# A weighted sum of two experts' rows: all transfers in one queue, in a fixed order

## The chip, the cores and the metric

The kernel runs on one core of a Trainium2 chip. The metric is the device time in microseconds (us), as the median of several executions. The span in a profile is the time from the first to the last instruction of one profiled execution, and is a little shorter than the device time.

Five engines can work side by side on a core. Three matter here: VectorE (DVE in the profile), ScalarE (ACT), and SyncE (SP), which computes nothing and issues transfers. A transfer (DMA) between the large memory (HBM, "dram" in the profile) and the on-chip memory (SBUF, 128 partitions) is put into the queue of the engine that issues it, and is carried out by the core's 16 DMA engines. An instruction that issues a transfer first waits until what it needs is there: a load until its buffer is free, a store until its result is computed. While it waits, the instructions behind it on the same engine wait too.

## The reference

```python
batch, seq, hidden, n_experts, k = 16, 1024, 512, 8, 2
expert_outputs   # (16, 1024, 2, 512) float32
combine_weights  # (16, 1024, 2)      float32

def reference(expert_outputs, combine_weights):
    weights = combine_weights[..., np.newaxis]
    return np.sum(expert_outputs * weights, axis=2).astype(np.float32)
```

There are 16 x 1024 = 16,384 tokens. Each has two rows of 512 numbers, one from each of two experts, and two weights; the output row is the weighted sum. 67.1 MB are read and 33.6 MB are written.

## The kernel before

Each of the 128 partitions takes 128 tokens. They are worked in eleven tiles: ten of 12 tokens per partition (J) and one of 8 (LAST). A full tile is 128 x 12 x 1024 numbers, 6.29 MB to load; its result is half of that, 3.15 MB to store. The last tile is 4.19 MB to load and 2.10 MB to store. The result is written over the first half of the tile's own buffer, so that a buffer is free for the next load only when its store has landed. There are four buffers (`bufs=4`); tile g + 4 uses the buffer of tile g.

```python
J, LAST = 12, 8
main = per - LAST            # per = 128 tokens per partition
last = main // J             # 10: tiles 0 to 9 are full, tile 10 is the short one
wpool = ctx.enter_context(tc.tile_pool(name="w", bufs=1))
ipool = ctx.enter_context(tc.tile_pool(name="in", bufs=4))
wt = wpool.tile([P, per * k], dt)
# ... the weights are loaded by two small transfers, on SyncE's and ScalarE's queue

for g in range(last + 1):
    et = ipool.tile([P, J, k * h], dt)
    ot = et.rearrange("p j f -> p (j f)")[:, 0 : J * h].rearrange("p (j f) -> p j f", f=h)
    t0, c = g * J, J if g < last else LAST
    nc.sync.dma_start(out=et[:, 0:c], in_=eo(t0, c))                 # L67, the load
    if g < last - 1:                                                 # tiles 0 to 8
        wb = wt[:, g * J * k : (g + 1) * J * k].unsqueeze(2).to_broadcast([P, J * k, h])
        ek = et.rearrange("p j (k h) -> p (j k) h", k=k)
        nc.vector.tensor_tensor(out=ek, in0=ek, in1=wb, op=mult)     # L72
        nc.vector.tensor_tensor(out=ot, in0=et[:, :, 0:h], in1=et[:, :, h : 2 * h], op=add)  # L73
        nc.scalar.dma_start(out=o(t0, c), in_=ot)                    # L74, the store, ScalarE's queue
        continue

    for i in range(c):                                               # tiles 9 and 10
        t = t0 + i
        nc.scalar.activation(                                        # L80, first row times its weight
            out=et[:, i, 0:h], in_=et[:, i, 0:h], func=copy, scale=wt[:, 2 * t : 2 * t + 1]
        )
        if g == last:                                                # tile 10
            nc.vector.scalar_tensor_tensor(...)                      # L84, second row times weight, plus first
    if g < last:                                                     # tile 9
        # ... x1 is the tile's second rows, w1 their weights
        nc.vector.tensor_tensor(out=x1, in0=x1, in1=w1.to_broadcast([P, c, h]), op=mult)  # L95
        nc.vector.tensor_tensor(out=ot, in0=et[:, :, 0:h], in1=x1, op=add)                # L96
    nc.sync.dma_start(out=o(t0, c), in_=ot[:, 0:c])                  # L97, the last two stores, SyncE's queue
```

So there are eleven loads in SyncE's queue, nine stores in ScalarE's, and two stores in SyncE's behind all loads. A framework sets the waits between the instructions.

Of the kernel before, what the change touches and what calls it, by code (L numbers as in the profile page):

```python
# [1 line left out]

# [4 lines left out]


@with_exitstack
def kernel(  # L10
    ctx: ExitStack,
    tc: tile.TileContext,
    expert_outputs: bass.AP,
    combine_weights: bass.AP,
    out: bass.AP,
):

    nc = tc.nc  # L20
    b, s, k, h = expert_outputs.shape
    assert k == 2
    n = b * s
    P = nc.NUM_PARTITIONS
    per = n // P
    assert per * P == n
    J, LAST = 12, 8
    main = per - LAST
    assert main % J == 0
    eo = expert_outputs.rearrange("b s k h -> (b s) (k h)")  # L30
    cw = combine_weights.rearrange("b s k -> (b s) k")
    o = out.rearrange("b s h -> (b s) h")

    def rows(x):

        a = x[0 : P * main, :].rearrange("(p t) f -> p t f", p=P)
        b = x[P * main : n, :].rearrange("(p t) f -> p t f", p=P)
        return lambda t, c: a[:, t : t + c, :] if t < main else b[:, t - main : t - main + c, :]

    eo, cw, o = rows(eo), rows(cw), rows(o)  # L40

    dt = mybir.dt.float32
    mult = mybir.AluOpType.mult
    add = mybir.AluOpType.add
    copy = mybir.ActivationFunctionType.Copy

    last = main // J

    wpool = ctx.enter_context(tc.tile_pool(name="w", bufs=1))
    ipool = ctx.enter_context(tc.tile_pool(name="in", bufs=4))  # L50

    wt = wpool.tile([P, per * k], dt)

    for eng, t, c in ((nc.sync, 0, main), (nc.scalar, main, LAST)):
        eng.dma_start(  # L55
            out=wt[:, k * t : k * (t + c)].rearrange("p (t k) -> p t k", k=k), in_=cw(t, c)
        )

    warm = wpool.tile([P, 1], dt)
    nc.scalar.activation(out=warm, in_=nc.const_aps.tensor(1.0, (P, 1), dt), func=copy)  # L60

    for g in range(last + 1):
        et = ipool.tile([P, J, k * h], dt)

        ot = et.rearrange("p j f -> p (j f)")[:, 0 : J * h].rearrange("p (j f) -> p j f", f=h)
        t0, c = g * J, J if g < last else LAST
        nc.sync.dma_start(out=et[:, 0:c], in_=eo(t0, c))  # L67
        if g < last - 1:

            wb = wt[:, g * J * k : (g + 1) * J * k].unsqueeze(2).to_broadcast([P, J * k, h])  # L70
            ek = et.rearrange("p j (k h) -> p (j k) h", k=k)
            nc.vector.tensor_tensor(out=ek, in0=ek, in1=wb, op=mult)  # L72
            nc.vector.tensor_tensor(out=ot, in0=et[:, :, 0:h], in1=et[:, :, h : 2 * h], op=add)  # L73
            nc.scalar.dma_start(out=o(t0, c), in_=ot)  # L74
            continue


        for i in range(c):
            t = t0 + i
            nc.scalar.activation(  # L80
                out=et[:, i, 0:h], in_=et[:, i, 0:h], func=copy, scale=wt[:, 2 * t : 2 * t + 1]
            )
            if g == last:
                nc.vector.scalar_tensor_tensor(  # L84
                    out=ot[:, i, :],
                    in0=et[:, i, h : 2 * h],
                    scalar=wt[:, 2 * t + 1 : 2 * t + 2],
                    in1=et[:, i, 0:h],
                    op0=mult,
                    op1=add,  # L90
                )
        if g < last:
            w1 = wt.rearrange("p (t k) -> p t k", k=k)[:, t0 : t0 + c, 1:2]
            x1 = et[:, :, h : 2 * h]
            nc.vector.tensor_tensor(out=x1, in0=x1, in1=w1.to_broadcast([P, c, h]), op=mult)  # L95
            nc.vector.tensor_tensor(out=ot, in0=et[:, :, 0:h], in1=x1, op=add)  # L96
        nc.sync.dma_start(out=o(t0, c), in_=ot[:, 0:c])  # L97


# [1 line left out]
_INS = ['expert_outputs', 'combine_weights']  # L101
_OUTS = [((16, 1024, 512), 'float32')]


# [23 lines left out]
```

## Time and profile before

| | before |
|---|---|
| device time, median of three (lowest to highest) | 240.05 us (239.09 to 240.25) |
| the profiled execution: device time; span | 239.26 us; 237.5 us |
| VectorE busy | 194.0 us (82%), 28 instructions |
| ScalarE busy | 14.0 us (6%), 22 instructions |
| moved by DMA | 100.80 MB, mean 424 GB/s over the span |
| a full load, median from issue to landing | 29.9 us |
| a store in ScalarE's queue, median from issue to landing | 33.2 us |

An engine's busy time is the time in which it works on instructions; issuing a transfer is not counted. For transfers there are two ways to look. "From issue to landing" is the whole time that one transfer takes, the time spent behind and beside others included. The share of the DMA engines tells how full the 16 of them are in a stretch of time, whoever issued what. In a line of groups, "L72" is a line of the kernel's file, "et<-et,wt" what is written and read, "x9" the count, and then come the busy time in all and the mean in ns of one.

### The profile page before, as it was taken

To read this page: it belongs to the slowest core of one execution; us is meant where nothing else is said; L and a number is where in the kernel's file an instruction comes from. 1 tells how busy PE (TensorE), PEld (TensorE's weight loads), DVE (VectorE), ACT (ScalarE), POOL (GpSimd) and SP (SyncE) were. 2 spreads that over 40 slices of the span, in tenths; PEclk is the share of its full clock that TensorE was granted. 3 is DMA by queue.
4 is the path that set the end of the run, shared out by engine and by line. 5 is a ranking of instruction groups with operands and counts; after the bars stand their busy time and mean duration, and the time that the engine had idled before them with its cause. 6 is when DMAs were issued, how large, how long until landed. Compare 5 with 4: busy or idle time off the path is not lost.

```text
span 237.5 us, 153 instructions
## 1 busy us (share of the span) xinstructions
DVE 194.0 (82%) x28; ACT 14.0 (6%) x22; POOL 0.2 (0%) x4
## 2 busy tenths in 40 slices
DVE  0008999999999999999999879969996998785710
ACT  2000000000000000000000000000000000740800
POOL 0000000000000000000000000000000000000000
DMA  8999999889899999999898999999998989999997
GB/s 287 397 488 439 397 414 505 381 364 522 356 439 431 430 464 464 397 397 505 356 522 364 439 431 430 464 464 397 397 505 356 513 368 443 447 414 442 422 417 309
DMA packets 3456, 100.80 MB, mean 424 GB/s; under 512 B 512, under 2 KB 640, under 8 KB 640
## 3 DMA queue, kind: packets, MB, share of 16 engines
q1 hardware_dynamic: 2016, 72.48, 71.2%
q10 hardware_dynamic: 1440, 28.32, 27.7%
HBM read 67.24 MB, written 33.55 MB: 424 GB/s over the span
## 4 chain that ended last, share of the span: by engine, by line
DMA 59%; DVE 33%; ACT 2%; DVEq 0%; ACTq 0%; issue 0%; SPq 0%
DMA et<-in_expert_outputs_dram 30%; DMA out_dram<-et 29%; DVE et L72 22%; DVE et L73 11%; ACT et L80 2%; DVE et L84 1%; DVEq L123 0%; ACTq L123 0%; SPq L55 0%; SPq L67 0%; DVEq L72 0%; ACTq L80 0%
## 5 line engine op out<-in xcount | busy, mean ns | idle before, releaser
L72 DVE TENSOR_TENSOR et<-et,wt 128x12288 f32<-128x12288 f32 x9 | 116.6, 12955 | 25.3 <-DMA et<-in_expert_outputs_dram 25.3
L73 DVE TENSOR_TENSOR et<-et 128x6144 f32<-128x6144 f32 x9 | 59.0, 6558 | 0.3
L80 ACT ACTIVATE et<-et,wt 128x512 f32<-128x512 f32 x20 | 12.5, 708 | 210.0 <-DMA et<-in_expert_outputs_dram 210.0
L84 DVE SCALAR_TENSOR_TENSOR et<-et,wt 128x512 f32<-128x512 f32 x8 | 5.6, 747 | 3.9 <-ACT et L80 3.7
L95 DVE TENSOR_TENSOR et<-et,wt 128x6144 f32<-128x6144 f32 x1 | 6.6, 6558 | 2.2 <-DMA et<-in_expert_outputs_dram 2.2
L96 DVE TENSOR_TENSOR et<-et 128x6144 f32<-128x6144 f32 x1 | 6.6, 6558 | 0.9 <-ACT et L80 0.9
L60 ACT ACT_TABLE_LOAD x1 | 1.3, 1283 | 1.2 <-PEq L112 1.2
L60 ACT ACTIVATE warm<-const-float32-1.0 128x1 f32<-128x1 f32 x1 | 0.2, 203 | 0.0
L112 POOL MEMSET const-bfloat16-1.0<- 128x1 bf16 x1 | 0.1, 102 | 0.0
L112 POOL MEMSET const-uint8-127<- 128x1 uint8 x1 | 0.1, 102 | 0.0
L112 POOL MEMSET const-float32-0.0<- 128x1 f32 x1 | 0.1, 99 | 0.2 <-issue 0.2
L112 POOL MEMSET const-float32-1.0<- 128x1 f32 x1 | 0.1, 99 | 0.0
## 6 DMA issues: line engine op xcount, KB each, us to landing
et<-in_expert_outputs_dram SPq DMA_DIRECT2D x10, 6144.0 KB, 29.9
out_dram<-et ACTq DMA_DIRECT2D x9, 3072.0 KB, 33.2
et<-in_expert_outputs_dram SPq DMA_DIRECT2D x1, 4096.0 KB, 25.1
out_dram<-et SPq DMA_DIRECT2D x1, 3072.0 KB, 14.7
out_dram<-et SPq DMA_DIRECT2D x1, 2048.0 KB, 10.0
wt<-in_combine_weights_dram SPq DMA_DIRECT2D x1, 120.0 KB, 2.1
wt<-in_combine_weights_dram ACTq DMA_DIRECT2D x1, 8.0 KB, 2.3
```

Source lines behind the costliest of these rows:

```text
L60: nc.scalar.activation(out=warm, in_=nc.const_aps.tensor(1.0, (P, 1), dt), func=copy)
L72: nc.vector.tensor_tensor(out=ek, in0=ek, in1=wb, op=mult)
L73: nc.vector.tensor_tensor(out=ot, in0=et[:, :, 0:h], in1=et[:, :, h : 2 * h], op=add)
L80: nc.scalar.activation(out=et[:, i, 0:h], in_=et[:, i, 0:h], func=copy, scale=wt[:, 2 * t : 2 * t + 1])
L84: nc.vector.scalar_tensor_tensor(out=ot[:, i, :], in0=et[:, i, h : 2 * h], scalar=wt[:, 2 * t + 1 : 2 * t + 2], in1=et[:, i, 0:h], op0=mul ...
L95: nc.vector.tensor_tensor(out=x1, in0=x1, in1=w1.to_broadcast([P, c, h]), op=mult)
L96: nc.vector.tensor_tensor(out=ot, in0=et[:, :, 0:h], in1=x1, op=add)
L112: nc = _bacc.Bacc("TRN2", target_bir_lowering=False, num_devices=1)
```

## The change

All loads and stores go into SyncE's one queue. The program issues four loads (one for each buffer), then the stores of tiles 0 and 1, and from there a load and a store by turns. The load of tile g + 3 stands behind the store of tile g; the buffer that it fills was that of tile g - 1, whose store stands two transfers earlier. `keep_in_program_order` keeps the framework from reordering the transfers. The computation is the same. The purpose is that transfers run one after another in an order that is known, each with the DMA engines to itself, and that a load waits for a store that has landed by the time it is to run, instead of one that still shares the DMA engines with other loads.

```diff
-    J, LAST = 12, 8
+    J, LAST, BUFS = 12, 8, 4
...
-    ipool = ctx.enter_context(tc.tile_pool(name="in", bufs=4))
+    ipool = ctx.enter_context(tc.tile_pool(name="in", bufs=BUFS))
...
-    for g in range(last + 1):
+    tiles = {}
+
+    def load(g):
+        t0, c = g * J, J if g < last else LAST
         et = ipool.tile([P, J, k * h], dt)
 
         ot = et.rearrange("p j f -> p (j f)")[:, 0 : J * h].rearrange("p (j f) -> p j f", f=h)
-        t0, c = g * J, J if g < last else LAST
-        nc.sync.dma_start(out=et[:, 0:c], in_=eo(t0, c))
+        tiles[g] = (t0, c, et, ot)
+        tc.keep_in_program_order(nc.sync.dma_start(out=et[:, 0:c], in_=eo(t0, c)))
+
+    def store(g):
+        t0, c, et, ot = tiles[g]
+        tc.keep_in_program_order(nc.sync.dma_start(out=o(t0, c), in_=ot[:, 0:c]))
+
+    def compute(g):
+        t0, c, et, ot = tiles[g]
         if g < last - 1:
...
-            nc.scalar.dma_start(out=o(t0, c), in_=ot)
-            continue
+            return
...
-        nc.sync.dma_start(out=o(t0, c), in_=ot[:, 0:c])
+
+    for g in range(BUFS):
+        load(g)
+    for g in range(last + 1):
+        compute(g)
+        store(g)
+        if 1 <= g <= last - BUFS + 1:
+            load(g - 1 + BUFS)
```

Nothing of the computation of a tile is changed but its place in the file: it now stands in `compute`.

## The prediction

> **What bounds the kernel now.** I read the page's slices and its part on DMA queues first, because this kernel moves 100.8 MB and multiplies little. The lines are the busy tenths and the GB/s of 40 equal slices, and then one line for each DMA queue: packets, MB, and the share of the span in which the 16 DMA engines worked for it. q1 is SyncE's queue, q10 ScalarE's.
>
> ```profile
> DVE  0008999999999999999999879969996998785710
> DMA  8999999889899999999898999999998989999997
> q1 hardware_dynamic: 2016, 72.48, 71.2%
> q10 hardware_dynamic: 1440, 28.32, 27.7%
> ```
>
> 71.2 + 27.7 = 98.9% of 237.5 us, that is 234.9 us, are DMA work. Only 237.5 - 234.9 = 2.6 us are left, and no digit of the DMA row is under 8 before the last. VectorE has more free time: it is busy for 82%.
>
> Next I asked for stretches of time. Each line has start:end and length, then the busy time of three engines, and as its last two numbers the DMA share and the GB/s. In order: loads alone, loads and stores mixed, nearly the whole time from the first to the last landing of a load, and the end.
>
> ```profile
> 3.00:38.00 35.00, 19.53 (x3) 0.00 (x0) 0.00 (x0) 1.00 0.99 427
> 157.00:195.00 38.00, 33.54 (x5) 0.00 (x0) 0.00 (x0) 1.00 1.01 435
> 18.40:220.00 201.60, 188.40 (x20) 7.46 (x12) 0.00 (x0) 1.00 1.00 430
> 236.00:237.50 1.50, 0.00 (x0) 0.00 (x0) 0.00 (x0) 1.00 0.00 0
> ```
>
> A share of 1.00 over 201.6 us means that no DMA engine stands idle there. (Short stretches scatter: the page's slices of 6 us go from 356 to 522 GB/s in the middle of the run, so only long ones are compared.) Loads alone and a mixture run at about one rate, 427 and 435 GB/s.
>
> Last I read what seems to contradict this: who waited for whom (us in total, times, longest), first in SyncE's queue and then for VectorE.
>
> ```profile
> SPq L67 <- DMA out_dram<-et: 174.1, 7, 45.8
> ```
>
> ```profile
> DVE et L72 <- DMA et<-in_expert_outputs_dram: 25.3, 5, 18.4
> ```
>
> And three pieces of the chain of waits (start, length, what):
>
> ```profile
> 1.17 17.17 DMA et<-in_expert_outputs_dram
> ...
> 76.94 30.80 DMA out_dram<-et
> ...
> 107.80 29.93 DMA et<-in_expert_outputs_dram
> ```
>
> SyncE waits 174.1 us ahead of seven loads for the stores that free their buffers, and VectorE 25.3 us for loads; a store of 3 MB takes 30.8 us, and the load that it releases 29.9 us more. That looks like latency to be cut. But each is long because others share the DMA engines with it: the first load, which has them nearly to itself, lands in 17.17 us. It is a chain of shared bandwidth.
>
> **What the Trainium skill says.** The page "DMA: Bandwidth & Descriptors", section "Issuing engines are not separate DMA queues", says that DMAs started from SyncE and ScalarE run on the same 16 DMA engines and interleave, and that a second issuing engine saves only the time of issuing. The trace agrees: the shares of the two queues add to 98.9%, not to more. The same page, "Queues, rings and completion order", says that a DMA engine takes turns between its queues packet by packet, and works within one queue in ring order. The trace agrees as far as it shows it: beside loads a store takes a median 33.2 us to land (page, DMA issues), though its bytes alone need about 7.3 us by the rate below. Its section "Where 436 GB/s comes from" gives a ceiling of 435.2 GB/s for these 16 engines; the mixed stretch above shows 435, so there is no speed above the present one to be found by order alone.
>
> **The change part by part.**
>
> *Removed and added work: none.* The same 11 loads, 11 stores and 2 loads of weights are issued, and the 28 VectorE and 22 ScalarE instructions stay. The nine stores move from ScalarE's queue to SyncE's, at 0.34 us of issuing each (timeline), 9 x 0.34 = 3.1 us spread over 200 us in which SyncE waits anyway. ScalarE loses 3.1 us of issuing, and is busy for 14.0 us of 237.5: no effect on the end. One real thing goes: the store of the ninth tile, whose add ended at 194.31 + 6.56 = 200.87, was issued at 203.18 because ScalarE stood at an activation waiting for the next load. 2.3 us, but the DMA engines were full then, so it bought nothing before and gives nothing now.
>
> *Moved: the order of transfers.* I calibrate on the kernel before. The first load landed at 18.34 (1.17 + 17.17). The last store was issued at 226.65 (timeline) and landed 10.0 us later (page): 236.65. Between them 100.66 - 6.29 = 94.37 MB landed in 218.3 us: 432.3 GB/s. So a load of 6.29 MB costs 14.55 us, a store of 3.15 MB 7.28, the short last load of 4.19 MB 9.70, its store of 2.10 MB 4.85. In one queue they come one after another: L0 L1 L2 L3 S0 S1 L4 S2 L5 S3 L6 S4 L7 S5 L8 S6 L9 S7 L10 S8 S9 S10. If nothing holds the queue up, they land at:
>
> L0 18.3, L1 32.9, L2 47.4, L3 62.0, S0 69.3, S1 76.5, L4 91.1, S2 98.4, L5 112.9, S3 120.2, L6 134.7, S4 142.0, L7 156.6, S5 163.8, L8 178.4, S6 185.7, L9 200.2, S7 207.5, L10 217.2, S8 224.5, S9 231.8, S10 236.6.
>
> *Does anything hold it up?* A transfer must be issued before the one ahead of it ends. VectorE takes 12.96 + 6.56 = 19.5 us for a tile (groups of lines L72 and L73), so tiles 0 to 3 are ready to be stored at 38.0, 57.5, 76.9 and 96.4; S0 to S3 get their turn at 62.0, 69.3, 91.1 and 112.9. Tiles 4 to 6 follow at 115.9, 135.4 and 154.9, for turns at 134.7, 156.6 and 178.4. From there the loads set the pace: tile 7 is ready at 156.6 + 19.5 = 176.1 (turn 200.2), tile 8 at 178.4 + 19.5 = 197.9 (turn 217.2). Tile 9 costs 7.5 us of ScalarE and one add of 6.6: 200.2 + 14.2 = 214.4 (turn 224.5). The last tile needed 226.65 - 220.01 = 6.6 us from landing to issue: 223.8 (turn 231.8). The loads: L4 must wait for S0's landing at 69.3 and has its turn at 76.5; each later load is issued a whole load and store before its turn. The tightest three are L4 with 7.2 us, S10 with 8.0 and S9 with 10.1. The cost of starting is bounded by the first load, 17.17 - 14.55 = 2.6 us. It fits into each, so the queue should never run empty.
>
> *Sum:* removed 0, added 0, DMA time the same 218.3 us after the first load, front (18.3) and end (237.5 - 236.65 = 0.9) unchanged. Span 237.5 us.
>
> **The rivals.**
>
> *A gain from shorter waits.* Loads now land in about 22 us instead of 30, and VectorE's waits can change places. If the chain were latency, each of the two chains store-load (30.8 + 29.9 and 37.4 + 25.1 us) would shrink by a fifth or more and the kernel by tens of us. Against it stands the DMA share of 1.00: at most the 2.6 us without DMA work can go, 1.1%. It would be 237.4 us at the very best, and those 2.6 us are the first issue, the first latency and the last landing, which the change keeps.
>
> *A loss at the head of the queue.* A store whose tile is late blocks every load behind it. By the slack above this needs a compute step 8 us late; for the tiles in the middle 14 us and more. If L4 alone came late, it would cost what exceeds 7.2 us, once: 241 to 244.
>
> *A loss or a gain by direction.* Sixteen engines now all load, then all store, with some 18 changes of direction in the queue. If each drained the engines for half a microsecond, the sum would be 9 us: 249. Against: before, two queues alternate load and store packets with a share of 1.01 at 435 GB/s. But there the second queue may be what hides the change, which one queue does not have; nothing in the trace tests a change of direction within one ring under load. A gain is as unlikely, as loads alone ran no faster than the mixture.
>
> **Range and chances.** The sum is zero. The median of the kernel before is 240.05 us, the profiled execution lasted 239.26 for a span of 237.5; the three runs spread over 1.2 us. I take 239.9, a hair under, since one cause of irregular packets, two queues on an engine, goes. The range of 238.9 to 241.3 holds the spread of the runs and half a microsecond of holes; it is wider above, because both losses are open upward and the gain is closed at 2.6. Within 2% (235.3 to 244.9) lies all but a costly change of direction: 0.95. Faster by over 2% would need a DMA rate above anything seen here: 0.01. Slower by over 2%: 0.04, the third rival nearly alone.
>
> **What would show it.** Right: one queue with about 98.9% share, the other near zero; S0 landing near 69 us and not 71, L4 near 91, and a load in mid-run landing within 22 us of its predecessor; a DMA share of 1.00 from 18 to 236 us; VectorE idle before tiles 7, 8 and 9 by about 2 us each; the wait of SyncE for stores mostly gone over to waits for VectorE and for earlier landings, and still a span of 237 to 238. Wrong: slices of the DMA row below 9 in the middle (the queue ran empty; the wait of SyncE that ends there names which), or a full DMA share at fewer GB/s (direction costs within packets), or a full share at more GB/s than 435 (order does change the rate).

## The result, and the profile after

The changed kernel takes 243.5 us (median of six executions, 242.64 to 244.35), the kernel before 240.18 us (six, 239.09 to 241.15). The ratio is 1.0134, with a 95% interval of 1.0098 to 1.0169: 3.3 us slower. The range of the prediction ended at 241.3.

The first profile after (span 242.6 us) is of the slowest of the six, so a second was taken (run `e10_changed_again` below). First the page's slices and its DMA queues:

```profile
DMA  8999999999899899999999899899999999999991
GB/s 273 421 486 397 430 470 397 446 454 397 373 421 494 389 409 434 446 438 397 462 413 470 353 458 462 381 434 474 438 385 474 438 389 417 439 417 439 434 415 57
q1 hardware_dynamic: 3312, 100.79, 97.4%
q10 hardware_dynamic: 144, 0.01, 0.0%
```

All transfers are in one queue. The DMA row is as full as before until the last slice, and there is a 1 with 57 GB/s. The page's shares give a first split of the loss: 97.4% of 242.6 us is 236.3 us of DMA work for the same bytes, against 234.9 before. So 1.4 us were added to the work, and the other 3.7 of the span's 5.1 us are time in which DMA engines stand idle. Where they stand idle is seen in stretches of time (start:end, length, busy time of three engines, clock, DMA share, GB/s). The kernel after:

```profile
18.40:230.00 211.60, 193.97 (x28) 12.46 (x20) 0.00 (x0) 1.00 1.00 428
236.00:237.00 1.00, 0.00 (x0) 0.00 (x0) 0.00 (x0) 1.00 0.73 311
237.00:238.00 1.00, 0.00 (x0) 0.00 (x0) 0.00 (x0) 1.00 0.23 98
238.00:239.00 1.00, 0.00 (x0) 0.00 (x0) 0.00 (x0) 1.00 0.11 49
239.00:240.00 1.00, 0.00 (x0) 0.00 (x0) 0.00 (x0) 1.00 0.08 33
240.00:241.50 1.50, 0.00 (x0) 0.00 (x0) 0.00 (x0) 1.00 0.05 22
```

The end of the kernel before, for comparison:

```profile
235.00:236.00 1.00, 0.00 (x0) 0.00 (x0) 0.00 (x0) 1.00 0.84 360
236.00:236.40 0.40, 0.00 (x0) 0.00 (x0) 0.00 (x0) 1.00 0.01 0
```

Up to 230 us the share is 1.00: the queue never ran empty. But after 236 us it falls in steps, 0.73, 0.23, 0.11, 0.05. One engine of 16 is a share of 0.06: for the last microseconds two engines work, and then one. I call this the thin end. Before, all 16 ended together within a microsecond.

The waits went where they were meant to go. In SyncE's queue (us in total, times, longest):

```profile
SPq L76 <- DVE et L85: 124.1, 9, 19.6
SPq L72 <- DMA out_dram<-et: 53.7, 7, 12.8
```

The seven loads wait 53.7 us for stores instead of 174.1, and the queue waits for VectorE instead. It helped nothing. Pieces of the chain of waits (start, length, what):

```profile
1.16 17.94 DMA et<-in_expert_outputs_dram
...
77.71 24.16 DMA out_dram<-et
101.88 37.36 DMA et<-in_expert_outputs_dram
...
190.62 31.74 DMA et<-in_expert_outputs_dram
```

The store of tile 2 lands in 24.2 us, the load behind it takes 37.4, because each is now issued earlier and stands in the queue longer. (The prediction said that loads "now land in about 22 us"; its own list has the load of tile 6 issued at 98.4, when the store of tile 2 lands, and landing at 134.7, which is 36.) The load of tile 6 lands at 101.88 + 37.36 = 139.2, where the prediction had 134.7, and the last load at 190.62 + 31.74 = 222.4 instead of 217.2. A transfer has landed when the slowest of the 16 engines has done its part.

**The packets.** The trace also records each packet with its length in time, and this shows both losses at once. A load's packet is one row of 49,152 bytes (8 for each engine and load); over nine in ten take 1815 ns to within 20 ns, and a store's packet of 24,576 bytes takes 912 ns, alone or mixed. I counted as slow what took over 20 ns more than the median of its size, summed the surplus and divided by 16, which gives us per engine. The thin end is the time for which an engine, on average, already stands idle when the last packet ends, less the 0.25 us of the kernel before.

| | slow at the first load | slow at the first turn to stores | slow later | thin end | last packet ends |
|---|---|---|---|---|---|
| before | 0.73 | 0.63 | 0.0 | 0.0 | 236.3 |
| after, first profile | 0.84 | 0.74 | 1.2 | 3.6 | 241.4 |
| after, second profile | 0.78 | 1.07 | 1.35 | 2.5 | 240.8 |

The second profile's execution took 243.71 us, the one before's 239.26; the difference of 4.45 is that of the last packets, 240.8 - 236.3. In both kernels the first packets are slow, and once more when the first stores begin. Only in the changed kernel does it go on: at nearly every later turn of the queue from a load to a store, the load's last packets are slow. In the first profile the turns after the loads of tiles 5 and 6 cost 0.3 us each on average, the others 0.03 to 0.2; in the second the dearest cost 0.5, and the one after tile 7 nothing. And it falls unevenly. The trace does not name a packet's engine, but each packet starts where another one ended, and joined in this way they make 16 chains, each with the same 176 packets (6.29 MB). In the first profile 14 of them end at 236.5 to 237.7, one at 239.6 and one at 241.4; the last had lost 1.6 us in the first load, 1.5 in the fourth and 1.25 in the fifth, where the mean was 0.84, 0.74 and 0.17. In the second profile ten end by 237.7, and six are spread from 238.0 to 240.8.

So the questions for the experiments: is it the one queue, its turns, the order of the program, or long stretches in which all engines do the same thing; and does it need writes to HBM?

### The profile page after: what moved, and what is told of

Same layout as the page of the kernel before. It is cut to its first block, busy times and chain, and to the rows that moved or that the text cites. A ratio compares the mean times of both kernels' runs of the same rounds, so it can differ in the third digit from the quotient of the medians.

```text
span 242.6 us, 148 instructions
## 1 busy us (share of the span) xinstructions
DVE 194.0 (80%) x28; ACT 14.0 (6%) x22; POOL 0.2 (0%) x4
## 3 DMA queue, kind: packets, MB, share of 16 engines
q1 hardware_dynamic: 3312, 100.79, 97.4%
## 4 chain that ended last, share of the span: by engine, by line
DMA 59%; DVE 33%; ACT 2%; DVEq 0%; ACTq 0%; issue 0%; SPq 0%
DMA et<-in_expert_outputs_dram 36%; DMA out_dram<-et 23%; DVE et L84 21%; DVE et L85 11%; ACT et L91 2%; DVE et L95 1%; DVEq L141 0%; ACTq L141 0%; SPq L55 0%; DVEq L84 0%; ACTq L91 0%
## 6 DMA issues: line engine op xcount, KB each, us to landing
out_dram<-et SPq DMA_DIRECT2D x1, 2048.0 KB, 12.7
```

## The experiments

Theory A: long stretches in one direction. Theory B: a single queue pays at each turn, which two queues hide. Rival C: the new program order itself.

**One line undone: the stores in ScalarE's queue.**

```diff
-        tc.keep_in_program_order(nc.sync.dma_start(out=o(t0, c), in_=ot[:, 0:c]))
+        tc.keep_in_program_order(nc.scalar.dma_start(out=o(t0, c), in_=ot[:, 0:c]))
```

> The changed program with one line altered: all eleven stores go to ScalarE's queue, the loads stay in SyncE's. Loads and stores mix packet by packet again. Theory A (long stretches in one direction: when all DMA engines turn from loads to stores together, the last load packets are slow, unevenly, and an engine that is late stays late) and theory B (one queue: an engine with a single queue pays at each change, with two it does not) both expect 240, with no thin end. Rival C (the new order of the program itself, or where it is kept, costs the time) expects 243 to 244.

Measured: 240.12 us, ratio 0.9998 (0.9983 to 1.0012). C falls: order and bookkeeping cost nothing. All of the loss comes from putting the stores into the loads' queue. The slow packets after the first turn to stores are gone (0.0), and the thin end is 0.7 us:

```profile
236.00:238.00 2.00, 0.00 (x0) 0.00 (x0) 0.00 (x0) 1.00 0.04 16
```

**Halves in one queue, and halves in two queues that turn together.** Each transfer is cut in two by tokens; in the first run both halves go to SyncE's queue, in the second one half to each.

```diff
-        tc.keep_in_program_order(nc.sync.dma_start(out=et[:, 0:c], in_=eo(t0, c)))
+        hc = c // 2
+        for i, eng in enumerate((nc.sync, nc.scalar)):      # control: (nc.sync, nc.sync)
+            tc.keep_in_program_order(
+                eng.dma_start(out=et[:, i * hc : (i + 1) * hc], in_=eo(t0 + i * hc, hc))
+            )
...                                                          # stores likewise
```

> A control for the next run: the changed kernel with each load and store cut into two transfers of half the tokens, all in SyncE's queue, same order. Packets are half as long. Both theories expect the time of the changed kernel plus something for the shorter packets, 243.5 to 246, with a thin end of 3 to 5 us.

> As the run before, but the first half of each transfer goes into SyncE's queue and the second into ScalarE's, in the same order. Each DMA engine has two queues to take turns between, yet both queues load at the same time and store at the same time. Theory A (long stretches in one direction) expects the time of the one-queue halves, within 1 us. Theory B (one queue) expects 3 us less than those, near the kernel before.

Measured: one queue 244.07 us, ratio 1.0153 (1.0122 to 1.0185); two queues 247.17 us, ratio 1.0298 (1.026 to 1.0337). B falls: with two queues to take turns between, but both loading and then both storing, it is slower still. That it takes 3.1 us more than the control is not what A expected (within 1 us). The long stretch of each kernel shows what kind of loss it is. One queue:

```profile
18.40:230.00 211.60, 193.88 (x28) 12.69 (x20) 0.00 (x0) 1.00 1.01 429
238.00:240.00 2.00, 0.00 (x0) 0.00 (x0) 0.00 (x0) 1.00 0.11 45
240.00:242.00 2.00, 0.00 (x0) 0.00 (x0) 0.00 (x0) 1.00 0.03 12
```

Two queues:

```profile
88.00:102.00 14.00, 14.00 (x3) 0.00 (x0) 0.00 (x0) 1.00 0.93 365
18.40:230.00 211.60, 190.79 (x25) 12.58 (x20) 0.00 (x0) 1.00 1.00 419
238.00:240.00 2.00, 0.00 (x0) 0.00 (x0) 0.00 (x0) 1.00 1.02 430
240.00:242.00 2.00, 0.00 (x0) 0.00 (x0) 0.00 (x0) 1.00 1.00 426
```

The one queue keeps its rate (429 GB/s) and loses at a thin end of 3.4 us. The two queues end together (0.1 us) and lose rate in the middle: 419 GB/s, with 4.1 us of slow packets per engine after the first turn to stores, against 0.3. Two things set this run apart from its control. Of the 4.1 us, 1.6 are in store packets, against less than 0.1 in the control. And VectorE worked in another order (two multiplications, then two additions), so that the store of tile 2 was issued at 91.55 only, and both queues had run empty ahead of it: the share of 0.93, 1.5 us per engine in all. B stays refuted, as it expected 3 us less than the control. But the two runs do not measure what two queues cost in long stretches. That the same disturbance shows as slow packets for all where engines stay in step, and as a few late engines where they do not, is an argument that fits; no run isolates it.

**Fewer turns: two loads and two stores at a time.**

```diff
         store(g)
-        if 1 <= g <= last - BUFS + 1:
-            load(g - 1 + BUFS)
+        if g % 2 == 1:
+            for n in (g + 3, g + 4):
+                if n <= last:
+                    load(n)
```

> The changed kernel, one queue, with two loads and two stores by turns: five turns from loads to stores instead of eight, each stretch twice as long in the middle. If the cost is a fixed one for each turn (either theory), the excess of 3.3 us falls to about 2: 242. If it grows with the length of the stretch, or is set by the first turns, it stays at 243 to 244. If the queue runs empty anywhere: more, with a DMA share under 1 in the middle.

Measured: 241.92 us, ratio 1.0058 (1.0037 to 1.0079). Five turns instead of eight leave 1.8 us over before instead of 3.3; the slow packets after the first turn to stores are 0.5 us instead of 1.2, the thin end 1.8. This fits a cost for each long stretch, not one that grows with its length. (Single executions range from 239.9 to 242.73.)

**Quarters in one queue: in long stretches, and mixed.** Each transfer is cut in four. The control keeps the order of the changed kernel; the other run puts one quarter of a load and one quarter of a store by turns, for tiles 4 to 10.

```diff
+    for g in range(2, last - 1):
+        n = g + 2
+        compute(g)
+        take(n)                      # the buffer of tile n
+        turns = "LLSLLSSS" if n == last else "LSLSLSLS"
...                                   # L: load(n, next quarter), S: store(g, next quarter)
```

> A control for the next run: the changed kernel, one queue, the same order, but each load and store is cut into four transfers of a quarter of its tokens. The stretches in one direction are as long as in the changed kernel, the packets a quarter as long. The halves had cost the full packets about 1.5 us more of DMA work (packet lengths in the trace), so quarters should cost 4.5. Both a cost of long stretches (A) and a cost of each turn of the queue (B) expect 240.2 + 4.5 and some 1 to 3 us of excess: 246 to 248, with a thin end.

> One queue and the same quarters, but in the middle of the run one quarter of a load and one quarter of a store by turns: four times as many turns from loads to stores as in the control, in stretches a quarter as long. A (long stretches in one direction make the last loads slow) expects 1 to 3 us less than the control, near 240.2 + 4.5 = 244.7, and a shorter thin end. B (each turn in one queue costs 0.4 us or so by itself) expects some 24 more turns to cost 5 us or more on top of the control.

Measured: in stretches 247.61 us, ratio 1.0303 (1.0274 to 1.0333); mixed 243.56 us, ratio 1.0153 (1.0113 to 1.0193). With four times the turns in the middle, in the same single queue with the same packets, it is 4.05 us faster, more than the 1 to 3 us that A expected. B falls a second time, and from the other side: a turn in one queue is not dear by itself; a turn after a long stretch is. In the trace of the mixed run all but 0.06 us of the slow packets after the first load lie between 75 and 90 us, where the last long stretch of stores (tiles 0 and 1) gives way to the mixture; 0.8 us in sum, and no packet that starts between 90 and 190 us adds more than 0.01. In the control, slow packets after 95 us add 0.8 us. The end of the control and then of the mixed run:

```profile
240.00:242.00 2.00, 0.00 (x0) 0.00 (x0) 0.00 (x0) 1.00 0.17 70
242.00:244.00 2.00, 0.00 (x0) 0.00 (x0) 0.00 (x0) 1.00 0.09 37
```

```profile
240.00:242.00 2.00, 0.00 (x0) 0.00 (x0) 0.00 (x0) 1.00 0.12 47
242.00:244.00 2.00, 0.00 (x0) 0.00 (x0) 0.00 (x0) 1.00 0.02 8
```

The mixed run has a thin end too, 2.7 us against 4.1 of the control; as its packets lose nothing after 90 us, its late engines were late by then. But its profile is of the slowest of its executions (245.6 us, the other three 243.11 to 243.64), and the two profiled executions differ by 1.8 us only. Where the rest of the 4.05 us lies, no trace shows. Both runs pay for short packets: quarters take 4 x 460 ns for a load row instead of 1815 and 4 x 234 for a store row instead of 912. The packets' medians sum to 237.1 us per engine instead of 232.75; as packets of one engine overlap a little at the borders of transfers, the engines are busy for 3.6 us longer than before, about what the mixed run's median is over before (3.4).

**Loads alone.** All computation and all stores but the last tile's are left out.

```diff
     for g in range(last + 1):
-        compute(g)
-        store(g)
-        if 1 <= g <= last - BUFS + 1:
-            load(g - 1 + BUFS)
+        load(g)
+    compute(last)
+    store(last)
```

> One queue, loads alone: the computation and the stores of tiles 0 to 9 are left out (so most of the output is not written), the last tile is computed and stored. 67.1 MB at 432 GB/s are 155.3 us, so the last load lands at 159 us and the device time is about 173. If the turns are at fault (A and B), there is none before the last load: the 16 DMA engines go on together and the DMA share is 1.00 up to the last load's end, with under 1 us of thin end. If DMA engines drift apart in one queue by themselves, the last load's end is thin over 3 us or more.

Measured: 174.52 us. Stretches of time up to the last load's end:

```profile
18.00:150.00 132.00, 0.00 (x0) 0.00 (x0) 0.00 (x0) 1.00 1.00 431
156.00:157.00 1.00, 0.00 (x0) 0.00 (x0) 0.00 (x0) 1.00 0.84 360
157.00:158.00 1.00, 0.00 (x0) 0.00 (x0) 0.00 (x0) 1.00 0.38 164
158.00:159.00 1.00, 0.00 (x0) 0.08 (x1) 0.00 (x0) 1.00 0.01 0
```

The last tile's computation starts at 158.92, as the loads' rate says (159). After the first load no load packet is slow. So the DMA engines did not drift apart in one queue by themselves; the edge at 157 to 158 is about as wide as one packet (1.8 us).

**The stores stay on the chip.** The stores of tiles 0 to 9 write to the free half of their own buffer, so most of the output is not written. Queue, order, turns and bytes stay.

```diff
-        tc.keep_in_program_order(nc.sync.dma_start(out=o(t0, c), in_=ot[:, 0:c]))
+        to = et.rearrange("p j f -> p (j f)")[:, J * h : 2 * J * h].rearrange("p (j f) -> p j f", f=h)
+        to = o(t0, c) if g == last else to[:, 0:c]
+        tc.keep_in_program_order(nc.sync.dma_start(out=to, in_=ot[:, 0:c]))
```

> The changed kernel, one queue, same order and same bytes, but the stores of tiles 0 to 9 write to the free second half of their own buffer in SBUF instead of to HBM, so most of the output is not written; only the last tile is stored. The DMA engines turn from long stretches of one kind of transfer to another as before, but HBM is only read. If writing to HBM in long stretches is what slows the loads at a turn, the slow load packets and the thin end go: at most 240, with the DMA engines ending within 1 us of each other. If the change from one kind of transfer to another in the DMA engine or its queue is the cause, they stay: 243 to 244 with a thin end of 3 us or more. (A copy within SBUF may itself run at another rate than a store; then only the thin end counts.)

Measured: 240.25 us, ratio 1.0012 (0.9999 to 1.0025), 0.25 us over the 240 that was expected at most if the writes are the cause. Stretches of time:

```profile
18.40:230.00 211.60, 193.88 (x28) 12.46 (x20) 0.00 (x0) 1.00 1.00 429
236.00:237.00 1.00, 0.00 (x0) 0.00 (x0) 0.00 (x0) 1.00 0.58 246
237.00:238.00 1.00, 0.00 (x0) 0.00 (x0) 0.00 (x0) 1.00 0.00 0
```

The thin end is gone (0.2 us), and no packet is slow after the first turn. A copy within SBUF takes 913 ns for a packet, a store to HBM 912, so the rate does not confuse the reading. The cost needs writes to HBM; turning the queue from one kind of transfer to another was free here. The first turn is still slow here (0.99 us), so that one is another cost, and what causes it is open: it comes once, in every kernel with full-size packets, whatever is written.

**A second profile of the changed kernel.**

> The changed kernel once more, for a second profile: its first profile is of its slowest execution. If the thin end is what costs most, it is there again, 2 to 4 us long, and the spans of the two profiles differ by about what their thin ends differ.

Measured: 243.71 us, span 241.9. The thin end is there again:

```profile
236.00:237.00 1.00, 0.00 (x0) 0.00 (x0) 0.00 (x0) 1.00 0.99 426
237.00:238.00 1.00, 0.00 (x0) 0.00 (x0) 0.00 (x0) 1.00 0.39 164
238.00:239.00 1.00, 0.00 (x0) 0.00 (x0) 0.00 (x0) 1.00 0.23 98
239.00:240.00 1.00, 0.00 (x0) 0.00 (x0) 0.00 (x0) 1.00 0.12 49
```

It is 2.5 us long instead of 3.6, with 0.4 us more of slow packets; the spans differ by 0.7.

**A try at a faster kernel.** The kernel before, with all weights loaded from ScalarE's queue.

```diff
-    for eng, t, c in ((nc.sync, 0, main), (nc.scalar, main, LAST)):
+    for eng, t, c in ((nc.scalar, 0, main), (nc.scalar, main, LAST)):
```

> The kernel before, with both loads of weights in ScalarE's queue, so that the first load of a tile is issued at once. SyncE's issue of the weights took 0.38 us ahead of it (chain of waits). As the DMA engines are full from the first packet to the last, an earlier first packet should shift the whole run: 0.4 us less than before, 239.8. If the weights' small packets now stand in the first load's way, or the engines' start does not depend on it, no change.

Measured: 239.91 us, ratio 0.9988 (0.9974 to 1.0001). The median moves by 0.25 us the right way, and the interval just includes no change. Not shown to be faster.

## Why the prediction was wrong

- *What bounds the kernel: right.* The DMA share stays 1.00 from 18.4 to 230 us in both kernels (431 GB/s before, 428 after). Cutting SyncE's wait for stores from 174.1 to 53.7 us gained nothing, and the rival of shorter waits falls.
- *The queue never runs empty: right.* The slack was enough; no head-of-line loss is seen.
- *The step that failed: the calibration.* "So a load of 6.29 MB costs 14.55 us, a store of 3.15 MB 7.28" took a rate from a kernel that mixes loads and stores packet by packet, and used it for long stretches. It also treats 16 DMA engines as one. "DMA time the same 218.3 us after the first load" is where this enters the sum; measured, from the first load's landing at 19.10 to the last store's at 229.0 + 12.7 = 241.7, it was 222.6. It failed in two terms. DMA work was taken as unchanged and grew by 1.4 us (234.9 to 236.3), nearly all of it at the later turns (1.2). And the end was taken as even: the thin end was 3.6 and 2.5 us in the two profiles. No sign of being wrong that the prediction lists looks at the end of the run. The prediction had S0 landing "near 69 us and not 71"; the load that waits for it was issued at 71.44.
- *The rival by direction: the right place, a wrong mechanism and a poor weight.* It had each of "some 18 changes" (its own list of transfers has 15) drain the engines for half a microsecond. A turn drained nothing (share 1.00) and was free as such (on-chip copies, mixed quarters). A turn from a long stretch of loads to a long stretch of HBM stores made the loads' last packets slow, 0 to 0.5 us on average after the first such turn, and up to 1.2 us in a single packet. The prediction wrote that "nothing in the trace tests a change of direction within one ring under load", and still kept its range to 1.4 us above the point. An untested term of up to 9 us asked for more.
- *"A hair under, since one cause of irregular packets, two queues on an engine, goes": the opposite.* Two queues, one with loads and one with stores, kept the packets regular: none was slow after the first turn.
- *The page leaned on.* That a second issuing engine saves only the time of issuing (the Trainium skill, "DMA: Bandwidth & Descriptors", "Issuing engines are not separate DMA queues") was taken to mean that two queues and one are the same for the rate. For loads beside stores the measurement decides otherwise: 240.12 us with two, 243.5 with one.
- *Still open.* Why HBM stores that all begin together slow the last loads, when as many mixed in slowed none after 90 us; and why the loss falls on a few engines. A late engine still loads while the others store, and so could become later; the losses of the last engine look like it, but no run tests it.

## What to carry to other kernels

When the DMA engines are full all the time, as here, shorter waits have nothing to give, and the queue's long waits are only shared bandwidth. Two queues, one for loads and one for stores, did more here than save issuing time: they mixed reads and writes packet by packet, and lining up the transfers in one queue lost that (1.3%; small pieces by turns in the one queue brought most of the mixture back, at the price of shorter packets). Look at the DMA share of the last microseconds: a fall in steps meant single late DMA engines here, which no busy row of the middle shows.

## What the runs showed of the hardware that was not expected

- A full share can hide a late engine: share 1.00 over 211.6 us, and then one to a few of 16 engines work until 2 to 5 us after the first have ended. Each of the 16 chains had the same 176 packets, so a late engine was not relieved by the others.
- The first turn from loads to stores costs 0.6 to 1.1 us per engine in every kernel here that stores full-size packets, even if the stores go to SBUF (0.99).
- Packets took 234, 460 and 912 ns for 6,144, 12,288 and 24,576 bytes, and 1815 for 49,152. A line through these has about 9 ns at zero bytes (an estimate from these four). Cut in four, the packets of this kernel summed to 237.1 us per engine instead of 232.75.
